# Streamed left operands of TensorE moved to multiples of 512 bytes: the pools of two projections of a decoder layer shifted and reordered

## The chip, the cores and the metric

The kernel runs on one core of a Trainium2 chip. The metric is the time of one execution in microseconds (us); three executions of the kernel before were timed, and their median stands for it.

## The reference

One decoder layer on 1024 tokens of width 1024, in float32, followed by a last RMSNorm:

```python
h = RMSNorm(x)
rnn_x, rnn_y, conv_B, conv_C, conv_x, gate_rnn, gate_conv = split(h @ w_in)   # 7 x 1024 columns
A = gelu(rnn_y) * RG_LRU(causal_conv4(rnn_x))     # two block-diagonal products in the gates
B = conv_B * causal_conv3(conv_C * conv_x)
x = x + (sigmoid(gate_rnn) * A + sigmoid(gate_conv) * B) @ w_out
x = x + (silu(n @ w_gate) * (n @ w_up)) @ w_down            # n = RMSNorm(x), hidden width 2816
x = x + sigmoid(RMSNorm(x) @ w_pg) * (p @ w_ple)
out = RMSNorm(x)
```

## The kernel before, in words

Every large product is done in float32 out of two halves: each operand is kept as a high and a low part (`split`, L83: ScalarE casts the high part, VectorE subtracts for the low one), and one product of tiles is three matmuls (`mm`, L108). Around this stands a scheme of seven block products instead of eight: the left matrix A and the right matrix B are cut into quarters, seven products of sums of quarters are made, and their results are added up in PSUM banks called X, Y and Z.

The stages follow one another: the transposed norm of x; the input projection, with the recurrence and the short convolution beside it; the output projection; gate and up; the down projection; the gate of the per-layer embedding and the last norm.

The input projection and gate/up are **streamed** (`stream`, L207). The weights are the left operand. They come in by DMA on SP's queue as quarters of 128x512 (`part`, pools `w1` and `w2`), are added up on VectorE (`source`, L232, with the tile `s1` of pool `ws`), cast by ScalarE (`high`, L248) and completed by VectorE (`low`, L253) into a tile `wop` of pool `wp` or, for the last two products of a later pair, of pool `wq`. The activations are the right operand: seven tiles of the pool `ops` made by `right_operands` (L173). They come from the norm of the second token half: `xt[4]` to `xt[7]` are scaled (L144), transposed on TensorE (L151, 32 transpositions), and VectorE and ScalarE read the transposed blocks (L190 and L192) into tiles `r` and `r_late`, out of which T1, T2, B22, T3 and -T4 are made (L86, L100). The two first products of the first four pairs need B11 and B21 alone, which are ready sooner; they run in front ("lead" products, 8 of 12 matmuls each). The first results are read out of PSUM into tiles of the pool `e0` (`z<-Z`, L514, in the input projection; `a<-Z`, L784, in gate/up); a bank comes free when that is done.

The output and down projections (`outer`, L336) have both operands in tiles of `ops`.

Where a tile lies in its partition follows from the pools: they are laid one behind the other in the order in which they are opened, behind what stays for the whole program. The pools of a stage (an `ExitStack`) take over the place of the pools of the stage before, and an instruction that writes a place waits for those that still use it. The stage before each stream has a `Frame` (L395) with pools `pq` (5 tiles of 8 KB), `pb` (4 of 4 KB: `xt[4]` to `xt[7]`), `pj`, `pa` (4 of 4 KB: `xt[0]` to `xt[3]`, then `r_late`) and `pr`, in that order. The table gives the places in bytes from the start of a partition.

| pool | before | rest to 512 | after | rest to 512 |
|---|---|---|---|---|
| Frame `pq` / `pb` / `pj` / `pa` | 132928 / 173888 / 190272 / 196416 | | the same | |
| `ops` (right operands everywhere; left ones in `outer`) | 17536 on | 128 | the same | 128 |
| `w1`, `w2`, `ws` | 132928 on | 320 | 133120 on | 0 |
| `wp`, 5 x 4096 | 153408 to 173888 | 320 | 153600 to 174080 | 0 |
| `wq`, 2 x 4096, gate/up | 190272 on | 320 | 174080 to 182272 | 0 |
| `wq`, input projection | 190400 on | 448 | 174080 to 182272 | 0 |
| `ev`, 4 x 2048 | 173888 on | 320 | 182272 on | 0 |
| `e0`, 4 tiles | 182080 on | 320 | 190464 on | 0 |

In the input projection the `e0` tiles are 2064 bytes, rounded to 2080; in gate/up 2048. The two block-diagonal products of the recurrence (`rg`) have their right operand `rg_w` in a tile of `wp` and their left one, `xo`, behind these pools; both go from rest 320 to 0 with the others.

The order in which a queue gets its instructions is the scheduler's: it simulates the program with the priorities of the code, so that another place, with other waits, can give another order.

Of the kernel before, what the change touches and what calls it, by code (L numbers as in the profile page):

```python
# [10 lines left out]
F32 = mybir.dt.float32  # L11
# [5 lines left out]
P = 128  # L17
T = 1024
D = 1024
H = 512  # L20
DFF = 2816
NF = DFF // P
EPS = 1e-6
LEAD = 4

# columns of the per-channel constants
C_W4, C_B4, C_BR, C_BI, C_LAM, C_W3, C_GM, C_GF, C_GP, NCST = 0, 32, 40, 48, 56, 64, 88, 96, 104, 112

# sections of the input projection
# [6 lines left out]
def kernel(ctx, tc, x, pT, w_in, w_gu, w_rg, w_out, w_down, w_pg, w_ple, cst, g_fin, out):  # L36
    """Float32 products run as float32r passes over exact 12-bit halves of the
    operands (lo*hi, hi*lo, hi*hi); the projections use Strassen's scheme in
    Winograd's form (seven block products in place of eight), whose running
    sums stay in PSUM:  # L40

        P1 = A11 B11    P2 = A12 B21    P3 = S4 B22    P4 = A22 (-T4)
        P5 = S1 T1      P6 = S2 T2      P7 = S3 T3
        S1 = A21 + A22  S2 = S1 - A11   S3 = A11 - A21   S4 = A12 - S2
        T1 = B12 - B11  T2 = B22 - T1   T3 = B22 - B12  -T4 = B21 - T2
        C11 = P1 + P2                   C12 = P1 + P6 + P5 + P3
        C22 = P1 + P6 + P7 + P5         C21 = P1 + P6 + P7 + P4

"""
# [33 lines left out]
    def split(hi, lo, src):  # L83
        """hi + lo == src, each with 12 significant bits."""
        nc.scalar.copy(hi, src)  # L85
        nc.vector.tensor_sub(lo, src, hi.bitcast(F32))  # L86

    def op_of(pieces, name):
        """A quarter of a matrix, given as pieces [P, k, H], as an operand."""
        t = ops.tile([P, 2, 4, H], F32R, tag="op", name=name)  # L90
        k = 0
        for q in pieces:
            n = q.shape[1]
            split(t[:, 0, k:k + n], t[:, 1, k:k + n], q)
            k += n
        return t
# [11 lines left out]
    def mm(ps, lhs, rhs, first, last, start):  # L108
        """ps (+)= lhs.T @ rhs; lhs and rhs give the two halves by index."""
        for n, (i, j) in enumerate(((1, 0), (0, 1), (0, 0))):  # L110
            nc.tensor.matmul(ps, lhs(i), rhs(j), start=start and first and n == 0,  # L111
                             stop=last and n == 2, skip_group_check=not start)

# [5 lines left out]
    root = [None]  # the last square root, behind which other tables may be loaded  # L119

    def rstd(ss, nb):
        """(sum of the parts / D + EPS) ** -0.5, with one Newton step behind the table."""
# [17 lines left out]
    def scale_rows(xt, y, spread):  # L140
        """xt[b] *= y[:, b]; spread: VectorE takes its share."""
        for b in range(4):
            if spread:
                nc.vector.tensor_scalar_mul(xt[b], xt[b], y[:, b:b + 1])  # L144
            else:
                nc.scalar.activation(xt[b], xt[b], AF.Copy, scale=y[:, b:b + 1])
# [7 lines left out]
    def norm_half(xt, ss, gc, piece, spread):  # L154
        """xt: four [P, D] tiles (overwritten), ss: their sums of squares. Returns the two quarters
        of (norm(x) * g).T for the first and second half of D, in pieces [P, 2, H]. spread: VectorE
        takes its share."""
# [15 lines left out]
    def right_operands(r11, r21, xt, ss, gc, piece, held=0):  # L173
        """The seven right operands in the order of use: B11, B21, T1, T2, B22, T3, -T4, from the
        quarters of the first token half and the blocks of the second (as for norm_half). The sums
        overwrite the quarters. held: so many banks of PSUM are taken for the products that follow
        before the transpositions take theirs."""
# [5 lines left out]
        second = []  # L183
# [20 lines left out]
    def stream_pools(st):  # L204
        return {n: pool(st, n, bufs) for n, bufs in (("w1", 4), ("w2", 4), ("ws", 2), ("wp", 5), ("ev", 4), ("e0", LEAD), ("wq", 2))}

    def stream(pools, srcs, hops, banks, take, pump=lambda: None, ahead=2, early=0):  # L207
        """srcs: raw rows of each pair of channel blocks. take(n)(blk, half, psum, sb): takes
        psum + sb, block blk of pair n on token half half. pump(): called behind each product."""
        n_pairs = len(srcs)  # L210
        # Two pairs run interleaved, so that a sum in PSUM is read three products before it goes
        # on; the first pairs run the products of the first token half in front.
# [11 lines left out]
        def part(q, i, j):  # L224
            """Quarter A(i, j) of pair q."""
            if (q, i, j) not in parts:
                t = pools["w%d" % i].tile([P, 4, P], F32, tag="w", name="part")
                dma[0] = nc.sync.dma_start(out=t, in_=srcs[q][i - 1][:, 4 * (j - 1):4 * j])
                parts[q, i, j] = t
            return parts[q, i, j]  # L230

        def source(q, i):  # L232
            """What becomes the left operand of product i of pair q; the sums overwrite the quarters."""
# [25 lines left out]
        def advance(n):  # L259
            """What is due before product n: the steps of an operand lie one product apart, the  # L260
            last ahead of its use by a few."""
# [48 lines left out]
    def deferred(work=()):  # L310
        """later(n, fn): fn runs n products from now (at once for 0). work: generators, of which
        the first goes a step with each product."""
# [23 lines left out]
    def outer(a, b, s1, nk, acc, after=lambda i: None, mid=lambda: None):  # L336
        """a, b: the four quarters of the operands as dicts of pieces (the sums overwrite them).
        after(i): called behind the results of product i."""
        def prep(i):
# [4 lines left out]
            if i == 5:  # L344
                each(add, s1, a[1, 0], a[1, 1])
                each(sub, b[0, 0], b[0, 1], b[0, 0])                       # T1
                return op_of(s1, "s1"), op_of(b[0, 0], "t1")
            if i == 6:
                each(sub, a[1, 0], a[0, 0], a[1, 0])                       # S3
                each(sub, a[0, 0], s1, a[0, 0])                            # S2  # L350
                each(sub, b[0, 0], b[1, 1], b[0, 0])                       # T2
                return op_of(a[0, 0], "s2"), op_of(b[0, 0], "t2")
            if i == 3:
                each(sub, a[0, 1], a[0, 1], a[0, 0])                       # S4
                return op_of(a[0, 1], "s4"), op_of(b[1, 1], "b22")
            if i == 7:
                each(sub, b[0, 1], b[1, 1], b[0, 1])                       # T3
                return op_of(a[1, 0], "s3"), op_of(b[0, 1], "t3")
            each(sub, b[1, 0], b[1, 0], b[0, 0])                           # -T4
# [28 lines left out]
    def load(pieces, src, r0, c0, eng=nc.sync):  # L388
        """src[r0:, c0:c0 + H] into pieces [P, k, H]."""
# [5 lines left out]
    class Frame:  # L395
        """Memory of the phases around a norm: tiles of x, quarters of its transposition, and
        quarters of the operands."""
# [32 lines left out]
    def residual(xt, ss, fr, last, store):  # L430
        """acc and after of outer: x += product; on the last round sums of squares, and the
        finished halves go out."""
# [20 lines left out]
    # ================= p @ w_ple; norm of x =================  # L453
    with ExitStack() as st:
# [5 lines left out]
        # pieces [P, 2, H] of [P, 2, 1024] by column halves  # L460
# [34 lines left out]
    # ================= input projection, recurrence, short conv =================  # L495
    with ExitStack() as st:
# [19 lines left out]
        def halo(sec, h, blk, width):  # L516
            """The columns before each half: zeros, then the end of the first half."""
# [7 lines left out]
        def recurrence(h):  # L525
            """In steps, one per product of the projection: what a step reads has been issued
            by the steps before it."""
            prev = [None, None]
            for half in range(2):
# [71 lines left out]
                for blk in range(2):  # L601
                    # 1 - a^2 = (1 + a^2) * tanh(-log a)
# [17 lines left out]
        def softplus():  # L620
            # 8 * softplus(-lambda) = 8 * (max(-lambda, 0) + log1p(exp(-|lambda|)))
# [9 lines left out]
            # log1p(e) = 2 atanh(s), s = e / (2 + e) <= 1/3  # L631
# [23 lines left out]
        def gate_v(h, blk, half):  # L655
            """conv * conv_b * sigmoid(gate), as the factors arrive."""
# [8 lines left out]
        def taker(h, sec):  # L665
# [22 lines left out]
            def use(t, *key):  # L688
# [12 lines left out]
                elif sec == GR:  # L701
                    hs = need(("h", *key))
                    # the next half still starts from the last column of this one
# [27 lines left out]
    # ================= output projection, residual, norm =================  # L731
# [36 lines left out]
    # ================= SwiGLU: gate and up =================  # L768
    with ExitStack() as st:
# [6 lines left out]
        def swiglu(f):  # L776
            def take(blk, half, psum, sb):
                # blk 0: gate, blk 1: up
# [21 lines left out]
    # ================= SwiGLU: down, residual, norm, ple gate, final norm =================  # L800
    with ExitStack() as st:
# [43 lines left out]
        def op_in_x(pieces, name):  # L845
            """An operand in the place of four tiles of x."""
# [13 lines left out]
        def gate(b, dh, left, cuts=1, last=False):  # L860
            """Token block b, half dh of the columns, in as many pieces as cuts."""
# [56 lines left out]
def _columns(a):  # L918
    """Per-channel rows [..., 1024] as columns [128, rows * 8]: channel = block * 128 + partition."""
# [4 lines left out]
def _pair_rows(w):  # L924
    """[1024, pairs, 2, 128] as [pairs, 2, 128 rows of a block, 8 blocks, 128 columns]."""
# [4 lines left out]
def _arrays(x, p, g_mix, w_in, conv4_w, conv4_b, w_rg_r, b_rg_r, w_rg_i, b_rg_i, lru_lambda, conv3_w, w_out,  # L930
# [4 lines left out]
    rg = np.stack([n(w_rg_r)[0], n(w_rg_i)[0]])  # [gate, head, i, j]  # L935
# [33 lines left out]
```

## Time and profile before

| | us |
|---|---|
| median of the three runs | 1463.45 |
| lowest, highest | 1461.16, 1463.68 |
| span of the profiled execution (first to last instruction) | 1458.2 |
| TensorE busy in it | 1437.6 |
| VectorE busy | 1077.8 |
| ScalarE busy | 781.7 |

The profile gives no time of the profiled execution other than its span. Its mean granted TensorE clock is 0.997. Times in the rows below are us from the start of that span. PE is TensorE's matmul, PEld its weight load, which overlaps the matmul before it; DVE is VectorE, ACT ScalarE. "idle before <-" names what an engine waited for. The end of a matmul is modelled, so the distance between two starts is the safer measure: from the first start of one row to the first start of the next, divided by the matmuls of the row.

### The profile page before, as it was taken

Reading aid. Unit: us, or ns where it says so; the run is one execution under the profiler, and the core shown is the slowest. Engines: PE = TensorE matmul, PEld = TensorE weight load, DVE = VectorE, ACT = ScalarE, POOL = GpSimd, SP = SyncE. Lnnn points to the kernel's source line nnn. Section 1 sums busy time; section 2 is a strip of 40 time slices with the busy share of each in tenths; the row PEclk is TensorE's granted clock in tenths of the full one; section 3 lists DMA queues with packets and bytes.
Section 4 is the critical chain, followed back from the end, with each engine's and each line's share of the span. In section 5 each row is a group of like instructions: output and inputs, shape, how many; then the busy total and the mean of one; then the engine's idle time right before and its main releaser. Section 6 shows DMA issues by size and latency. Waiting matters only on the chain.

```text
span 1458.2 us, 17521 instructions
## 1 busy us (share of the span) xinstructions
PE 1437.6 (99%) x6348; PEld 1176.0 (81%) x6348; DVE 1077.8 (74%) x1617; ACT 781.7 (54%) x1214; POOL 10.6 (1%) x20
## 2 busy tenths in 40 slices
PE   8999999999999999999999999999999999999997
PEld 6787888888888888878888888888888888888886
DVE  6989757965697669689796555555554899995854
ACT  7757746754775467545773333333333343346764
POOL 0000000000000000000000000000000000000000
PEclk9999999999999999999999999999999999999999
DMA  8321221122112211381522222222223761524431
GB/s 317 111 87 51 75 77 52 52 79 74 53 55 75 77 51 59 111 286 53 172 81 101 87 82 85 87 88 83 76 80 106 255 231 37 195 87 141 148 145 58
DMA packets 76742, 153.77 MB, mean 105 GB/s; under 512 B 7920, under 2 KB 7920, under 8 KB 76656
## 3 DMA queue, kind: packets, MB, share of 16 engines
q1 hardware_dynamic: 74768, 145.84, 29.9%
q0 software_dynamic: 1888, 6.82, 1.4%
q8 instruction: 50, 0.82, 0.2%
q14 instruction: 36, 0.29, 0.1%
HBM read 120.12 MB, written 32.51 MB: 105 GB/s over the span
## 4 chain that ended last, share of the span: by engine, by line
PE 90%; DVE 3%; DMA 3%; ACT 2%; issue 1%; SPq 0%; DVEq 0%; ACTq 0%
PE X L111 46%; PE Y L111 23%; PE Z L111 11%; PE pg L874 6%; PE rg L111 3%; PE tp L151 1%; DMA pe_d<-peo 1%; DMA xt<-x_d 1%; DMA xt<-in_x 0%; ACT b L85 0%; DVE a11b L100 0%; DMA act_d<-a 0%; DMA a<-m_d 0%; DMA m_d<-v 0%; DVE v L722 0%
## 5 line engine op out<-in xcount | busy, mean ns | idle before, releaser
L111 PE MATMUL X<-t,wop 128*128 128x512 f32 x1800 | 431.3, 393 | 0.0
L111 PEld LDWEIGHTS X<-t,wop 128*128 128x128 f32 x1800 | 338.2, 188 | 76.6 <-DVE wop L254 0.3
L250 ACT CAST wop<-part 128x512 fp32r<-128x512 f32 x300 | 183.7, 621 | 213.8 <-PE X L111 67.4
L254 DVE TENSOR_TENSOR wop<-part,wop 128x512 fp32r<-128x512 f32 x300 | 204.8, 689 | 89.0 <-ACT wop L250 87.8
L111 PE MATMUL Z<-b,wop 128*128 128x512 f32 x600 | 146.7, 393 | 0.4 <-ACT r_late L192 0.4
L111 PE MATMUL X<-b,wop 128*128 128x512 f32 x600 | 147.0, 393 | 0.0
L111 PE MATMUL Y<-b,wop 128*128 128x512 f32 x600 | 146.4, 393 | 0.0
L111 PE MATMUL Y<-t,wop 128*128 128x512 f32 x600 | 146.2, 393 | 0.0
L111 PEld LDWEIGHTS Z<-b,wop 128*128 128x128 f32 x600 | 112.5, 188 | 26.8 <-ACT r_late L192 0.9
L111 PEld LDWEIGHTS Y<-b,wop 128*128 128x128 f32 x600 | 112.8, 188 | 25.5
L111 PEld LDWEIGHTS Y<-t,wop 128*128 128x128 f32 x600 | 112.8, 188 | 25.2
L111 PEld LDWEIGHTS X<-b,wop 128*128 128x128 f32 x600 | 112.6, 188 | 24.6
L874 PE MATMUL pg<-b,a 128*128 128x512 f32 (+1 forms) x408 | 88.4, 378 | 0.0
L111 PE MATMUL X<-t,s 128*128 128x512 f32 x360 | 85.8, 392 | 0.0
L874 PEld LDWEIGHTS pg<-b,a 128*128 128x128 f32 x408 | 73.4, 188 | 14.6
L254 DVE TENSOR_TENSOR wop<-s,wop 128x512 fp32r<-128x512 f32 x50 | 34.5, 689 | 59.5 <-ACT wop L250 59.5
L111 PEld LDWEIGHTS X<-t,s 128*128 128x128 f32 x360 | 66.8, 188 | 13.9 <-DVE t L86 0.5
L271 ACT COPY p<-Y 128x512 f32<-128x512 f32 x50 | 29.2, 583 | 72.6 <-PE Y L111 72.6
L271 ACT COPY s<-X 128x512 f32<-128x512 f32 x50 | 29.2, 588 | 59.2 <-PE X L111 58.9
L271 ACT COPY u<-X 128x512 f32<-128x512 f32 x50 | 29.2, 584 | 49.6 <-PE X L111 49.1
L435 DVE TENSOR_TENSOR xt<-X,xt 128x512 f32<-128x512 f32 x64 | 43.8, 686 | 14.5 <-PE X L111 13.6
L111 PE MATMUL rg<-xo,rg_w 128*128 128x512 f32 x192 | 47.1, 393 | 0.1
(172 smaller groups left out, 1939.7 us busy)
## 6 DMA issues: line engine op xcount, KB each, us to landing
part<-in_w_in SPq DMA_DIRECT2D x120, 256.0 KB, 2.6
part<-in_w_gu SPq DMA_DIRECT2D x96, 256.0 KB, 2.7
act_d<-a SPq DMA_DIRECT2D x44, 256.0 KB, 2.4
x_d<-xt SPq DMA_DIRECT2D x32, 256.0 KB, 2.0
bc<-in_w_down SPq DMA_DIRECT2D x10, 512.0 KB, 5.8
a<-act_d SPq DMA_DIRECT2D x10, 512.0 KB, 5.9
xt<-in_x SPq DMA_DIRECT2D x8, 512.0 KB, 8.0
pe_d<-peo SPq DMA_DIRECT2D x16, 256.0 KB, 2.9
```

The lines of the kernel that those rows point to most:

```text
L111: nc.tensor.matmul(ps, lhs(i), rhs(j), start=start and first and n == 0, stop=last and n == 2, skip_group_check=not start)
L151: nc.tensor.transpose(ps[:, b * P:(b + 1) * P], xt[b][:, kk * P:(kk + 1) * P], ident)
L250: nc.scalar.copy(t[:, 0], s)
L254: sub(t[:, 1], s, t[:, 0].bitcast(F32))
L271: nc.scalar.copy(t, ps)
L435: add(piece, ps, piece)
L874: nc.tensor.matmul(ps, left[k // 4](i, k % 4)[:, c:c + P], right[k // 4, dh][:, j, k % 4, r], start=n + k == 0, stop=n == 2 and k == 7)
```

## The change

One pool of 192 bytes that nothing uses is opened ahead of the others, and `wq` is opened behind `wp` instead of last. (All comments were dropped too, so that lines behind L203 are two higher in the new file.)

```diff
     def stream_pools(st):
-        return {n: pool(st, n, bufs) for n, bufs in (("w1", 4), ("w2", 4), ("ws", 2), ("wp", 5), ("ev", 4), ("e0", LEAD), ("wq", 2))}
+        pool(st, "rest", 1).tile([P, 48], F32, name="rest")
+        return {n: pool(st, n, bufs) for n, bufs in (("w1", 4), ("w2", 4), ("ws", 2), ("wp", 5), ("wq", 2), ("ev", 4), ("e0", LEAD))}
```

No engine has an instruction more or fewer. Their order differs at the starts of the two streams. TensorE at the start of gate/up, before (`tp` is a bank with transposed blocks, `b_5936` is B11, `b_5941` B21, `t_5998` T1):

```order
L111 MATMUL X<-t_5659,a_5654 128x512 x43
L111 MATMUL X<-b_5936,wop 128x512 x22
L151 MATMUL tp<-ident,xt 128x128 x5
L111 MATMUL X<-b_5936,wop 128x512
L151 MATMUL tp<-ident,xt 128x128 x15
L111 MATMUL X<-b_5936,wop 128x512 x7
L151 MATMUL tp<-ident,xt 128x128 x4
```

and after the change (B11 is `b_5941` now, B21 `b_5946`, T2 `t_6038`, T1 `t_6003`):

```order
L111 MATMUL X<-t_5664,a_5659 128x512 x45
L151 MATMUL tp<-ident,xt 128x128 x32
L111 MATMUL X<-b_5941,wop 128x512 x12
L111 MATMUL Z<-b_5946,wop 128x512 x12
...
L111 MATMUL X<-t_6038,wop 128x512 x12
L111 MATMUL Y<-t_6003,wop 128x512 x12
```

The transpositions, which stood among the first products, stand ahead of them. VectorE at the same place, before:

```order
L137 SCALAR_TENSOR_TENSOR rz<-rt,ry 128x4
L254 TENSOR_TENSOR wop<-part,wop 128x512
L144 TENSOR_SCALAR xt<-xt,rz 128x1024 x4
L245 TENSOR_TENSOR part<-part 128x512
L190 SCALAR_TENSOR_TENSOR r<-tp,cs,r 128x512 x2
...
L254 TENSOR_TENSOR wop<-part,wop 128x512
L784 TENSOR_TENSOR a<-Z,s_6119 128x512
L190 SCALAR_TENSOR_TENSOR r<-tp,cs,r 128x512 x3
```

and after the change, with the first lo-halves of `wop` (L256 now) and, further down, the first sums out of PSUM (L786 now):

```order
L144 TENSOR_SCALAR xt<-xt,rz 128x1024 x4
L190 SCALAR_TENSOR_TENSOR r<-tp,cs,r 128x512 x4
L86 TENSOR_TENSOR t_6003<-r,t_6003 128x1024
L190 SCALAR_TENSOR_TENSOR r<-tp,cs,r 128x512 x2
L256 TENSOR_TENSOR wop<-part,wop 128x512 x4
...
L86 TENSOR_TENSOR b_6050<-r_late,b_6050 128x1024
L100 TENSOR_TENSOR r<-r 128x1024
L786 TENSOR_TENSOR a<-Z,s_6128 128x512
```

The first lo-half moved from ahead of the scaling of `xt` to behind six steps of L190, and the first `a<-Z` from among them to behind both halves of B22. At the start of the input projection VectorE makes the four `z` sums, which stood apart among the steps for T2, T3 and B22, in one row behind them:

```order
L86 TENSOR_TENSOR b_492<-r_late,b_492 128x1024 x2
L100 TENSOR_TENSOR r<-r 128x1024
L516 TENSOR_TENSOR z<-Z,s_574 128x512
L516 TENSOR_TENSOR z<-Z,s_614 128x512
L516 TENSOR_TENSOR z<-Z,s_665 128x512
L516 TENSOR_TENSOR z<-Z,s_702 128x512
```

There `b_492` is B22, and the order of TensorE's first products stays as it was.

## Rows read from the trace of the kernel before

**Rows 1.** The page, part 1: busy us, share of the span, instructions.
```profile
PE 1437.6 (99%) x6348; PEld 1176.0 (81%) x6348; DVE 1077.8 (74%) x1617; ACT 781.7 (54%) x1214; POOL 10.6 (1%) x20
```

**Rows 2.** The page, part 4: the chain that ended last, by engine.
```profile
PE 90%; DVE 3%; DMA 3%; ACT 2%; issue 1%; SPq 0%; DVEq 0%; ACTq 0%
```

**Rows 3.** Stretches in three stages: length, PE, PEld, DVE, ACT, POOL, clock, DMA, GB/s.
```profile
1180.00:1330.00 150.00, 150.00 (x663) 124.23 (x662) 143.97 (x156) 60.90 (x71) 5.76 (x8) 1.00 0.41 136
760.00:1150.00 390.00, 390.00 (x1706) 320.05 (x1705) 229.36 (x333) 144.60 (x244) 2.54 (x4) 1.00 0.30 98
150.00:620.00 470.00, 470.00 (x2032) 381.65 (x2031) 350.94 (x557) 283.90 (x441) 0.00 (x0) 1.00 0.21 69
```

**Rows 4.** Timeline of TensorE in the input projection: start, length, operation.
```profile
339.30 2.96 PE L111 MATMUL Y<-b,wop 128*128 128x512 f32 x12
342.10 5.76 PE L111 MATMUL X<-t,wop 128*128 128x512 f32 x24
347.70 2.96 PE L111 MATMUL Y<-t,wop 128*128 128x512 f32 x12
...
361.65 5.66 PE L111 MATMUL X<-t,wop 128*128 128x512 f32 x24
367.14 2.91 PE L111 MATMUL Y<-t,wop 128*128 128x512 f32 x12
```

**Rows 5.** The two streams in their steady parts, columns as in rows 3.
```profile
77.43:633.79 556.36, 556.21 (x2401) 451.05 (x2400) 421.75 (x684) 343.52 (x531) 1.56 (x2) 1.00 0.23 73
748.29:1143.81 395.52, 395.52 (x1729) 324.52 (x1728) 234.64 (x339) 148.20 (x249) 2.54 (x4) 1.00 0.29 94
```

**Rows 6.** Groups of weight loads: busy us, mean ns, idle before.
```profile
L111 PEld LDWEIGHTS Y<-t,wop 128*128 128x128 f32 x600 | 112.8, 188 | 25.2
L111 PEld LDWEIGHTS X<-t,s 128*128 128x128 f32 x360 | 66.8, 188 | 13.9 <-DVE t L86 0.5
```

**Rows 7.** Timeline of TensorE at the start of gate/up.
```profile
716.08 5.20 PE L111 MATMUL X<-b,wop 128*128 128x512 f32 x22
721.32 0.74 PE L151 MATMUL tp<-ident,xt 128*128 128x128 f32 x5
...
745.54 2.91 PE L111 MATMUL Y<-t,wop 128*128 128x512 f32 x12
```

**Rows 8.** Timeline of VectorE there.
```profile
716.28 0.69 DVE L435 TENSOR_TENSOR xt<-X,xt 128x512 f32<-128x512 f32 x1
...
719.82 0.69 DVE L254 TENSOR_TENSOR wop<-part,wop 128x512 fp32r<-128x512 f32 x1
720.43 2.73 DVE L144 TENSOR_SCALAR xt<-xt,rz 128x1024 f32<-128x1024 f32 x4
```

**Rows 9.** Timeline of ScalarE there.
```profile
728.01 1.06 ACT L85 CAST t<-r 128x1024 fp32r<-128x1024 f32 x1
```

**Rows 10.** Timeline of VectorE near 58 us, steps back to back.
```profile
58.00 0.69 DVE L243 TENSOR_TENSOR part<-part 128x512 f32<-128x512 f32 x1
58.60 1.22 DVE L100 TENSOR_TENSOR r_late<-r_late 128x1024 f32<-128x1024 f32 x1
59.73 0.69 DVE L254 TENSOR_TENSOR wop<-s,wop 128x512 fp32r<-128x512 f32 x1
```

**Rows 11.** Stretches before the first stream, columns as in rows 3.
```profile
38.00:41.00 3.00, 1.38 (x10) 1.07 (x11) 3.00 (x5) 1.64 (x4) 0.00 (x0) 0.99 0.93 326
41.00:44.30 3.30, 3.15 (x16) 2.67 (x15) 3.30 (x7) 2.56 (x6) 0.00 (x0) 0.50 0.26 99
```

**Rows 12.** Waits of TensorE: us in total, times, longest.
```profile
PE Z L111 <- DVE a L86: 2.1, 1, 2.1
```

**Rows 13.** Timeline of TensorE at the first `rg` product.
```profile
97.03 2.93 PE L111 MATMUL rg<-xo,rg_w 128*128 128x512 f32 x12
99.79 2.97 PE L111 MATMUL X<-t,wop 128*128 128x512 f32 x12
```

## The prediction, written before the result was known

> **What bounds the kernel now.** I read the page's busy times first, then the chain that ended last, then the stretches of TensorE one by one. TensorE is busy 99% of the span [rows 1] and holds 90% of the chain [rows 2]. So only two things can move the time: the distance from one matmul to the next, and places where TensorE has no product to start.
>
> The distance is not the same everywhere, and that is what the change is about. In the output and down projections (outer products, left operands in the `ops` pool) 662 weight loads stand in 150 us: 226.6 ns each. In gate/up 1705 stand in 390 us: 228.7 ns. In the input projection 2031 stand in 470 us: 231.4 ns [rows 3]. The clock is 1.00 in all three and the work is the same 128x512 matmul. What differs is where the left operand begins in its partition. By the sizes of the pools, an `ops` tile begins 128 bytes past a multiple of 512, a `wp` tile 320 bytes past one, a `wq` tile 320 past in gate/up but 448 past in the input projection, since there the four `z` tiles ahead of it are 2,064 bytes, rounded to 2,080. The right operands are the same `ops` tiles in all three. Row by row in the input projection, two products side by side run at 2.80 us per twelve matmuls (339.30 to 342.10, and 342.10 to 347.70 for 24): 233.3 ns; later ones at 5.49 us for 24 (361.65 to 367.14): 228.8 ns [rows 4]. By the operands that stand there, the slow period begins with products from `wq` and lasts over products from `wp` behind them until the next pair from `wq`. So the trace orders three places: 128 gives 226.6, 320 gives 228.8, 448 gives 233.3 and slows its neighbours. It shows no stream of 128x512 products at 0.
>
> **The change, part by part.** It adds and removes no instruction on any engine. It does two things.
>
> *The places.* All left operands of the two streams go to 0. The stretch from the first steady product of the input projection to the first outer product has 2400 weight loads in 556.36 us, 231.8 ns each; the one of gate/up has 1728 in 395.52 us, 228.9 ns each [rows 5]. Nothing in the trace prices place 0. The bounds: from above the 233.3 ns of the worst place (a loss of 2400 x 1.5 + 1728 x 4.4 = 11.2 us); from below a pace under all that the trace shows. The nearest row to that is the weight load's own duration, 188 ns [rows 6]; nothing comes near it, and a third of the way from 226.6 towards it (214) is as far as I would go, a gain of 4128 x 16.6 = 68 us. I take the value of place 128, 226.6 ns: the pace falls steadily from 448 over 320 to 128, place 0 is next to 128, and 226.6 is flat in its stretch, matmul after matmul, as if the place no longer mattered there. Gain: 2400 x 5.2 = 12.5 us, less 0.6 us of short stalls in that stretch which stay, so 11.9; and 1728 x 2.3 = 4.0 us. Together **-15.9 us**.
>
> *The order of the starts.* The pools also come to lie over other tiles of the stage before. Before, `wp` (20 KB) lay wholly over `pq`, whose tiles are done early. Now its fifth buffer reaches 192 bytes into `xt[4]`, and `wq` lies over `xt[4]` and `xt[5]`: weights for the first products wait until the second token half has been transposed. `e0` now lies over `pj` and the first `r_late` tile, so that the first sums out of PSUM wait until T3 and B22 have been made.
>
> At the start of gate/up, products on B11 began at 716.08, with the 32 transpositions let in between them, and the first Y followed at 745.54 [rows 7]. Now all 32 transpositions stand ahead of the first product. Chain: the last `xt` sum ends at 716.97; the scaling of `xt` starts at 720.43 behind a lo-half [rows 8], so at 719.8 without it, and takes 2.7; four steps of L190 take 2.6 more, to 725.2; then ScalarE's casts of t1 (1.06 us, [rows 9]), its `r_late` steps and the first `wop` cast, to 728.5, and the lo-half on VectorE, to about 729.4. TensorE meanwhile has only the transpositions, 13.3 us in place of products that took the same time before. Eight lead products at 2.72 us bring it to 751.2, the one on T2 to 753.9. Y needs a bank of PSUM, which comes free with the first `a<-Z` sum on VectorE. That one now stands behind ten 128x1024 steps, two of L190 and sixteen 128x512 ones counted from 731.0. Back to back the long and the short ones take 1.13 and 0.60 us [rows 10]: 11.3 + 1.3 + 9.6 = 22.2, to 753.2, and with 1.7 us, an estimate, for casts that ScalarE brings late, 754.9. Against 745.54 that is 9.4 us; I take **+10 us**, because the clock may be at half while TensorE only transposes: before the first stream, behind 3 us in which TensorE was busy for 1.38, it was 0.50 over 3.3 us of transpositions [rows 11], and such a stretch is 1.65 us of work lost. Bounds: 8.4 (TensorE's own chain, VectorE in time) less whatever slack I misjudged, say 5; and 13.3 + 1.7 = 15, nothing made good.
>
> At the start of the input projection the transpositions already stood ahead of the products, which start about where they did. There only the `z` sums move: all four now stand behind the lo-halves of T3 and B22 and the sums for T4. The first Y waits for them until about 72.2, with TensorE ready at 70.7. I take **+1.4 us**, between 0 and 3.
>
> At both ends of the streams, the loads of the next stage stand where they stood on SP's queue, or ahead of the last stores; TensorE's one wait there, 2.1 us for `a` [rows 12], hangs on the last `m_d` store and stays. Cost nothing; if that cover fails it is one load, under 3 us.
>
> **Sum:** -15.9 + 10 + 1.4 = -4.5 us. The profiled execution's span is 1458.2 us; the median of the runs is 1463.45, so some 5 us lie outside the span, and I take them as unchanged. 1463.45 - 4.5 gives **1459.0**.
>
> The Trainium skill bears on the first term. The page "TensorE: Matmul & The Clock Gate" (Part 2, step 1, LDWEIGHTS) says that the load of the left operand has a read port of its own and that its time depends on the number of columns alone. By that rule the start address changes nothing and the sum would be +11.4. The trace agrees for the load's own time, 188 ns in every group [rows 6], but the pace differs at the same columns and clock [rows 3], and there the measurement decides.
>
> **The rivals.**
>
> *The pace does not follow the place that way (slower).* Then only the starts are left: 1463.45 + 11.4 = 1474.9. For it: the correlation rests on three places, each in its own stage, and `rg`, whose two operands both begin at 320, takes 2.76 us per twelve (97.03 to 99.79), 230 ns [rows 13], about what `wp` has. What may count is the distance between left and right operand: 0 gives 226.6, 192 gives 228.8, 320 gives 233.3, and the change makes it 384, worse than all. `rg` at distance 0 but not at 226.6 speaks against that. At 233.3 everywhere: 11.2 more, 1486. The rival decides from the point where the pace gains no more than the starts lose: 11.4 us over 4128 matmuls, 2.8 ns, that is a mean of 227.8 against 230.6 before. Chance 0.22.
>
> *Place 0 is better than 128.* The 512 bytes of a weight load that begins on a multiple of 512 lie in one piece of that size; from place 128, as from 320 and 448, they lie in two. If the pace went to 220, another 4128 x 6.6 = 27 us: 1432. Against it: 226.6 is flat, and a price on the second piece would show at 128, 320 and 448 alike. Chance 0.16. The same page of the Trainium skill gives a gap of 512 / 2.4 + 2.5 = 216 ns between such matmuls (Part 2, "Back-to-back issue gap"); by it the time would be near 1415, and no row here shows that pace.
>
> *The starts cost nothing.* If VectorE catches up and TensorE's first products only move, -15.9 stands alone: 1447.6. Against it: 13.3 us of products have to come from somewhere, and TensorE has no idle time behind in which to make them good. Chance 0.08, within the forecast's 0.62 of a pace near 226.6.
>
> **How the numbers follow.** Forecast (pace 226 to 227, gate/up start 5 to 15): 0.62, 1454 to 1464. Pace rival above 0.22, pace rival below 0.16. The range runs from 1445 (the forecast with free starts and a little more pace) to 1475 (no gain in pace at all). It leaves out a pace well under 225 and one worse than now, together about 0.2. A measurement of this kernel tells about 0.2% from no change, 2.9 us. Faster by more: 0.16 and six tenths of the forecast's case, 0.53. Slower by more: nearly all of 0.22 and a little of the forecast, 0.24. The same: 0.23.
>
> **What would show it.** Right: in the profile of the changed kernel the stretches of both streams have one even distance near 226.6 ns, the input projection takes 12 us less than 556.36 and gate/up 4 less; TensorE shows 32 transpositions in a row near 722 to 729, the first product near 729 and Y near 755. Wrong: a distance of 228.8 or more with the operands at 0, which is the first rival; or products among the transpositions, which would make the starts cheaper than I say.

## The result and the profile after

The changed kernel takes 1485.08 us (median of four runs) where the kernel before took 1462.43 in the same comparison: a ratio of 1.0163, 95% interval 1.0148 to 1.0179. It is slower by 22.7 us; the forecast was 1459.0, that is 4.5 us faster.

The page of the changed kernel, span, parts 1 and 4, to set beside [rows 1, 2]:

```profile
span 1482.2 us, 17509 instructions
...
PE 1452.0 (98%) x6348; PEld 1179.5 (80%) x6348; DVE 1079.5 (73%) x1617; ACT 782.5 (53%) x1214; POOL 10.6 (1%) x20
...
PE 91%; DVE 4%; DMA 2%; ACT 1%; issue 1%; POOL 0%; SPq 0%; DVEq 0%; ACTq 0%
```

TensorE is the bound as before, and has become slower itself: 14.4 us more of busy time for the same 6348 matmuls. (The page of before counts 17521 instructions; each engine's own count is the same, the difference lies in instructions on semaphores.) The steady parts of the two streams (columns as in rows 3), to set beside [rows 5]:

```profile
78.08:637.36 559.28, 559.23 (x2402) 450.38 (x2400) 420.87 (x673) 342.50 (x529) 1.56 (x2) 1.00 0.23 72
765.70:1167.26 401.56, 401.56 (x1730) 325.55 (x1728) 230.51 (x335) 147.53 (x250) 2.55 (x4) 1.00 0.28 92
```

That is 233.0 ns a matmul in the input projection (231.8 before) and 232.4 in gate/up (228.9 before), at a clock of 1.00. The pace is not 226.6. Row by row in the input projection the fast stretches of [rows 4] are gone; product after product takes 2.80 us for twelve matmuls, 233.3 ns each:

```profile
343.95 5.76 PE L111 MATMUL X<-t,wop 128*128 128x512 f32 x24
349.55 2.96 PE L111 MATMUL Y<-t,wop 128*128 128x512 f32 x12
```

The start of gate/up on TensorE, to set beside [rows 7]:

```profile
712.84 10.49 PE L111 MATMUL X<-t,a 128*128 128x512 f32 x45
727.25 6.77 PE L151 MATMUL tp<-ident,xt 128*128 128x128 f32 x32 [3.92 <-DVE xt L144]
736.15 4.62 PE L111 MATMUL X<-b,wop 128*128 128x512 f32 x12 [2.12 <-DVE wop L256]
...
762.91 2.95 PE L111 MATMUL Y<-t,wop 128*128 128x512 f32 x12
```

The last product of the output projection ends at about 712.84 + 45 x 0.2267 = 723.04 (716.08 before, where the first `wop` product followed at once). All 32 transpositions stand alone, with idle time on both sides, and the granted clock falls with it: its mean is 0.57 over the transpositions and 0.62 over the first product behind them, so that most of both stretches was at the lower of its two levels, 0.50 (1.2 GHz):

```profile
722.00:727.25 5.25, 1.33 (x7) 0.79 (x5) 3.11 (x10) 1.13 (x5) 0.00 (x0) 0.91 0.26 100
727.25:734.10 6.85, 6.77 (x32) 5.82 (x32) 5.80 (x9) 3.66 (x6) 0.00 (x0) 0.57 0.00 0
...
736.15:740.60 4.45, 4.45 (x12) 3.50 (x13) 4.45 (x6) 3.37 (x6) 0.00 (x0) 0.62 0.71 214
```

Cut at the same places of the program, the 24.0 us between the two spans lie as follows:

| piece | before, us | after, us | difference |
|---|---|---|---|
| to the first steady product of stream 1 | 77.43 | 78.08 | +0.65 |
| stream 1, 2400 matmuls | 556.36 | 559.28 | +2.92 |
| output projection | 82.29 | 85.68 | +3.39 |
| start of gate/up | 32.21 | 42.66 | +10.45 |
| gate/up, 1728 matmuls | 395.52 | 401.56 | +6.04 |
| the rest | 314.35 | 314.95 | +0.60 |

The 3.39 us at the output projection were not expected. There GpSimd, ScalarE, VectorE, SP's queue and TensorE wait for one another in turn. It begins with the load of B21 of `w_out` (`b<-in_w_out`), which GpSimd issues. Before and after the change (the long wait is only that GpSimd has nothing else to do):

```profile
625.92 1.56 POOL L392 DMA_DIRECT2D b<-in_w_out  x2 [624.61 <-DMA bc<-in_w_out]
```

```profile
632.23 1.56 POOL L394 DMA_DIRECT2D b<-in_w_out  x2 [630.92 <-DVE b L86]
```

ScalarE of the changed kernel waits for that load to land:

```profile
634.31 1.03 ACT L85 CAST a<-a 128x1024 fp32r<-128x1024 f32 x1
639.65 1.05 ACT L85 CAST b<-b 128x1024 fp32r<-128x1024 f32 x1 [4.30 <-DMA b<-in_w_out]
641.71 1.05 ACT L85 CAST b<-b 128x1024 fp32r<-128x1024 f32 x1 [1.00 <-DMA b<-in_w_out]
642.66 0.62 ACT L687 ACTIVATE z<-z 128x512 f32<-128x512 f32 x1
```

And TensorE waits further down, in the kernel before and in the changed one:

```profile
652.45 5.73 PE L111 MATMUL Z<-b,a 128*128 128x512 f32 x24 [2.15 <-DVE a L86]
```

```profile
648.28 5.60 PE L111 MATMUL Z<-b,a 128*128 128x512 f32 x24
657.73 7.36 PE L111 MATMUL Z<-b,a 128*128 128x512 f32 x24 [3.85 <-DVE a L86]
```

By the sizes of the pools the load goes into the last tile of `pq`, at 165696. Before, that place was two `wop` buffers exactly; shifted by 192 bytes, the end of a third one lies in it too. The load was issued at 625.92 before, 7.87 us ahead of the stage's first product (633.79), and now 5.13 us ahead of it (632.23 against 637.36): 2.74 us later, about one product of 2.80. In both kernels the issue stands 0.47 us behind the start of a product of the stream, the third from the end before (625.45) and the second from the end now (631.76). That it waits for the product in front of that one is inferred from this; the profile names other steps as what ended the wait. ScalarE waits for it with the sigmoid of the last `z` (642.66) queued behind; so the last store to `m_d` and the load of `a` come late, and TensorE waits 3.85 us for it instead of the 2.1 of [rows 12]. Behind the gap 24 matmuls take 7.20 us (657.73 to 664.93, clock 0.76) instead of 5.57 (652.45 to 658.02, clock 1.00):

```profile
657.70:664.93 7.23, 7.20 (x24) 5.76 (x25) 5.54 (x8) 1.47 (x5) 0.00 (x0) 0.76 0.55 206
```

One correction to the part on the kernel: in the `rg` products `rg_w` is the left operand and `xo` the right one, and both lie in tiles of `wp`. So their distance is 0 in every kernel here.

### The profile page after: what moved, and what is told of

It reads as the page before. It is cut to its first block, busy times and chain, and to the rows that moved or that the text cites. A ratio compares the mean times of both kernels' runs of the same rounds, so it can differ in the third digit from the quotient of the medians.

```text
span 1482.2 us, 17509 instructions
## 1 busy us (share of the span) xinstructions
PE 1452.0 (98%) x6348; PEld 1179.5 (80%) x6348; DVE 1079.5 (73%) x1617; ACT 782.5 (53%) x1214; POOL 10.6 (1%) x20
## 4 chain that ended last, share of the span: by engine, by line
PE 91%; DVE 4%; DMA 2%; ACT 1%; issue 1%; POOL 0%; SPq 0%; DVEq 0%; ACTq 0%
PE X L111 47%; PE Y L111 23%; PE Z L111 11%; PE pg L876 6%; PE rg L111 3%; PE tp L151 1%; DMA pe_d<-peo 1%; DMA b<-in_w_out 1%; PE ple L111 1%; DMA prow<-in_pT 0%; DVE t L86 0%; DMA a<-m_d 0%; DVE xt L437 0%; DVE wop L256 0%; DVE v L724 0%
## 5 line engine op out<-in xcount | busy, mean ns | idle before, releaser
L256 DVE TENSOR_TENSOR wop<-part,wop 128x512 fp32r<-128x512 f32 x300 | 204.2, 689 | 94.3 <-ACT wop L252 92.8
L256 DVE TENSOR_TENSOR wop<-s,wop 128x512 fp32r<-128x512 f32 x50 | 34.5, 689 | 60.6 <-ACT wop L252 60.5
L111 PE MATMUL Z<-b,a 128*128 128x512 f32 x180 | 43.4, 400 | 3.9 <-DVE a L86 3.9
```

Of the source, the lines that this page charges most:

```text
L256: sub(t[:, 1], s, t[:, 0].bitcast(F32))
```

## The experiments

Below, the place of an operand is where it begins, in bytes past a multiple of 512. Theory A: the pace follows the distance from the right operand's place to the left one's. Theory B, the prediction's: it follows the left operand's own place. The streams and the outer products of before and after have four places of the left operand and only one of the right (128), so they can't tell. The right operands (and both operands of the outer products) can be moved without moving anything else: some or all of the 704 bytes of small tiles (pool `sm`) go ahead of `ops` instead of behind it, so that all behind them stays where it was. "z tiles of 2176" means that the early `z` tiles are padded, so that `wq` has the same place as `wp` in both streams.

**E1, all at 320.**

```diff
-    ops = ctx.enter_context(tc.tile_pool(name="ops", bufs=7))
     sm = ctx.enter_context(tc.tile_pool(name="sm", bufs=2))
+    ops = ctx.enter_context(tc.tile_pool(name="ops", bufs=7))
...
-            return (sp["e0"] if early else zp).tile([P, H + 4], F32, tag="z", name=name)
+            return (sp["e0"] if early else zp).tile([P, H + (32 if early else 4)], F32, tag="z", name=name)[:, :H + 4]
```

> The kernel before with the small pool opened ahead of the pool of the right operands, and early z tiles of 2176 bytes: all left and right operands of 128x512 products begin 320 past a multiple of 512, order of every engine as before. Theory A (the pace follows the distance from the right operand's place to the left one's, modulo 512; distance 0 is fast): 226.6 ns in both streams, about 1446.5 us. Theory B (the pace follows the left operand's own place): 228.8 ns in both streams and 228.8 instead of 226.7 in the outer products, about 1458.6 us.

Measured: 1445.85 us against 1460.17, ratio 0.9894 (0.9877 to 0.9911). The two streams:

```profile
75.28:620.50 545.22, 544.75 (x2401) 450.36 (x2400) 421.22 (x685) 342.20 (x531) 1.56 (x2) 1.00 0.23 74
735.25:1126.93 391.68, 391.68 (x1730) 324.43 (x1728) 234.88 (x339) 148.28 (x249) 2.55 (x4) 1.00 0.29 95
```

227.2 and 226.7 ns, in gate/up with the left operands exactly where they were. B falls. And the first `rg` product, whose operands have not moved at all against each other:

```profile
94.32 2.88 PE L111 MATMUL rg<-xo,rg_w 128*128 128x512 f32 x12
97.04 2.88 PE L111 MATMUL X<-t,wop 128*128 128x512 f32 x12
```

2.72 us for twelve, 226.7 ns, where [rows 13] show 2.76: there its neighbours were slow, here they are fast. Start by start, the trace of before shows the slow neighbour wear off within that product: the first distance is 240 ns, and from the eighth start to the twelfth (98.650 to 99.557) they stand 226.7 ns apart.

**E2, right operands at 448.** As E1, but only `rv`, `rs`, `ry`, `rt`, `rz` go ahead of `ops`:

```diff
-    ops = ctx.enter_context(tc.tile_pool(name="ops", bufs=7))
-    sm = ctx.enter_context(tc.tile_pool(name="sm", bufs=2))
+    sa, ops, sb = (ctx.enter_context(tc.tile_pool(name=n, bufs=b)) for n, b in (("sa", 2), ("ops", 7), ("sb", 2)))
+    sm = type("Small", (), {"tile": lambda *a, name, **k: (sa if name in ('rv', 'rs', 'ry', 'rt', 'rz') else sb).tile(*a, name=name, **k)})
```

> The kernel before with the right operands moved from 128 to 448 by putting some of the small tiles ahead of them, left operands of the streams all at 320, order of every engine as before. Distance 384, as after the change, but no tile lies over another one than before. Theory A: 232.4 to 233.3 ns in both streams, as after the change; 226.7 in the outer products, where both operands move together; about 1472 us. Theory B: 228.8 ns in the streams, 233 in the outer products, whose left operands are at 448; about 1466 us.

Measured: 1472.24 us, ratio 1.0077 (1.0058 to 1.0095).

```profile
78.23:637.44 559.21, 559.14 (x2401) 450.40 (x2400) 421.60 (x684) 344.34 (x531) 1.56 (x2) 1.00 0.22 73
752.08:1155.28 403.20, 403.20 (x1729) 324.38 (x1728) 235.31 (x339) 148.32 (x249) 2.54 (x4) 1.00 0.28 92
...
1200.00:1320.00 120.00, 120.00 (x532) 99.34 (x531) 117.47 (x126) 46.94 (x53) 4.33 (x6) 1.00 0.35 120
```

In the outer products (last row), whose two operands are at 448 here, 531 loads stand in 120 us, 226.0 ns, where theory B expected 233. The streams take 233.0 and 233.3 ns: the slow pace without any change to left operands, pools of the streams or order. This is the pace part of the loss by itself.

**E3, the order of the pools alone.**

```diff
-        pool(st, "rest", 1).tile([P, 48], F32, name="rest")
```

(taken out of the changed kernel).

> The changed kernel without the 192 bytes: wq ahead of ev and e0, left operands at 320 in both streams, right ones at 128 (distance 192). Both theories: 228.8 ns in both streams, 7 us less than before. If the new order of the pools alone makes the starts late (wq over xt[4] and xt[5], e0 over pj and the first r_late): first product of gate/up near 736 us, and about 14 us lost, 1469 us. If it is the 192 bytes by which wp reaches into xt[4]: products among the transpositions as before, about 1456 us.

Measured: 1456.55 us against 1460.17, ratio 0.9973 (0.9960 to 0.9987). TensorE at the start of gate/up:

```profile
708.20 5.20 PE L111 MATMUL X<-b,wop 128*128 128x512 f32 x22
713.44 0.73 PE L151 MATMUL tp<-ident,xt 128*128 128x128 f32 x5
...
741.15 3.03 PE L111 MATMUL Y<-t,wop 128*128 128x512 f32 x12 [0.57 <-DVE a L785]
```

Products stand among the transpositions as in [rows 7], the first 82.1 us behind the first outer product. The 0.57 us that Y waits for a sum of `a` is what the new place of `e0`, over `pj` and `r_late`, seems to cost. Stream 1 takes 550.70 us, 229.5 ns, now that `wq` is no longer at 448.

**E4, all at 0.** The changed kernel, split as in E2 with `ss` ahead of `ops` as well:

```diff
+    sm = type("Small", (), {"tile": lambda *a, name, **k: (sa if name in ('rv', 'rs', 'ry', 'rt', 'rz', 'ss') else sb).tile(*a, name=name, **k)})
```

> The changed kernel with the right operands moved from 128 to 0 as well: left and right operands of the streams and of the outer products all begin on multiples of 512; order of every engine as in the changed kernel. Theory A: 226.6 ns in both streams, 25 us less than the changed kernel, about 1460 us. Theory B: streams as in the changed kernel (232.4 to 233.3 ns), outer products slower too, about 1495 us.

Measured: 1461.6 us, ratio to before 1.0007 (0.9995 to 1.0019).

```profile
76.67:621.91 545.24, 544.75 (x2401) 450.22 (x2400) 420.27 (x673) 340.33 (x529) 1.56 (x2) 1.00 0.23 74
749.74:1141.50 391.76, 391.76 (x1730) 324.38 (x1729) 230.55 (x335) 147.89 (x250) 2.55 (x4) 1.00 0.29 94
```

Same left operands as in the changed kernel, same order on every engine, and a span that is 24.6 us shorter (1457.6). What is left is the late starts, paid for by the better pace.

**E5, the shift alone.** The old order of the pools, `z` tiles of 2176, and

```diff
     def stream_pools(st):
+        pool(st, "rest", 1).tile([P, 48], F32, name="rest")
```

> The kernel before with only the 192 bytes ahead of the streams' pools (and early z tiles of 2176 bytes, so that wq is at 0 too); the pools stay in their old order, so ev and e0 lie over xt and wq over pj and pa, as before. Left operands at 0, right ones at 128 (distance 384). Pace 232.4 to 233.3 ns in both streams. Theory S (the 192 bytes by which wp now reaches into xt[4], and the parts into the next tile, make the starts late): first product of gate/up behind all 32 transpositions, about 98 us behind the first outer product as in the changed kernel, about 1485 us. Rival (wq over xt and e0 over pj and r_late are needed for that as well): first product about 82 us behind it, as before, about 1471 us.

Measured: 1484.99 us, ratio 1.0171 (1.0149 to 1.0194), as slow as the changed kernel. TensorE:

```profile
728.87 6.77 PE L151 MATMUL tp<-ident,xt 128*128 128x128 f32 x32 [3.92 <-DVE xt L144]
737.77 4.61 PE L111 MATMUL X<-b,wop 128*128 128x512 f32 x12 [2.13 <-DVE wop L255]
```

The first product stands 98.7 us behind the first outer product (639.10). So the 192 bytes make this start late, and the new order of the pools is not needed for it.

**E6, E7, E8: how the distance counts.** As E2, left operands at 320, with other names in the list, so that the right ones are at 64, 256 and 384:

```diff
-    ... name in ('rv', 'rs', 'ry', 'rt', 'rz') ...
+    ... name in ('rv', 'rs', 'ry', 'rt', 'rz', 'fss') ...
+    ... name in ('rv', 'rs') ...
+    ... name in ('rv', 'rs', 'ry', 'rt') ...
```

> The kernel before with all left operands of the streams at 320 and the right ones at 64 (distance 256), order of every engine as before. If the distance counts modulo 256: 226.7 ns as at distance 0, about 1446 us. If it counts modulo 512: something else, between the 228.9 of distance 192 and the 233.3 of distance 320, about 231 ns, 1463 us.

```profile
737.35:1129.03 391.68, 391.68 (x1729) 324.32 (x1728) 234.62 (x339) 148.31 (x249) 2.55 (x4) 1.00 0.29 95
```

> The kernel before with all left operands of the streams at 320 and the right ones at 256 (distance 64), order of every engine as before. Modulo 256: 233.3 ns as at distance 320, about 1472 us. Modulo 512: next to distance 0, 226.7 to 228.9 ns, 1446 to 1455 us.

```profile
751.21:1154.41 403.20, 403.20 (x1730) 325.25 (x1728) 235.04 (x339) 148.40 (x249) 2.54 (x4) 1.00 0.29 92
```

> The kernel before with all left operands of the streams at 320 and the right ones at 384 (distance 448, or 64 the other way), order of every engine as before. Modulo 256: 228.9 ns as at distance 192, about 1455 us. Modulo 512: between the 233 of distance 384 and the 226.7 of distance 0, about 230 ns, 1460 us. If only the size of the gap counted and not its side, the same as at distance 64.

```profile
744.63:1140.14 395.51, 395.51 (x1729) 324.52 (x1728) 234.82 (x340) 148.34 (x249) 2.54 (x4) 1.00 0.29 93
```

Gate/up at 226.7, 233.3 and 228.9 ns, one run each of 1445.03, 1471.0 and 1456.06 us: all three as expected if the distance counts modulo 256.

**E10, E11: between the places.** Distances 32 and 224:

```diff
+    ... name in ('rv', 'rs', 'warm') ...
+    ... name in ('rv', 'rs', 'ry', 'rt', 'rz', 'fss', 'warm') ...
```

> The kernel before with all left operands of the streams at 320 and the right ones at 288 (distance 32), order of every engine as before. If the pace changes in steps of 64 bytes or more: 226.7 ns, 1445 us. If it changes smoothly: about 230 ns, between the 226.7 of distance 0 and the 233.3 of distance 64, 1459 us. If the best place is beside 0: below 226.7 ns.

```profile
753.60:1156.80 403.20, 403.20 (x1730) 324.65 (x1728) 235.20 (x339) 148.36 (x250) 2.55 (x4) 1.00 0.28 92
...
1200.00:1330.00 130.00, 130.00 (x576) 107.66 (x575) 127.06 (x136) 53.96 (x61) 4.34 (x6) 1.00 0.35 119
```

> The kernel before with all left operands of the streams at 320 and the right ones at 96 (distance 224), order of every engine as before. Steps of 64 bytes: 228.9 ns as at distance 192, 1456 us. Smooth: about 227.8 ns, 1451 us. If the best place is beside 0: below 226.7 ns.

```profile
754.72:1157.91 403.19, 403.19 (x1730) 323.84 (x1728) 234.94 (x339) 148.25 (x250) 2.54 (x4) 1.00 0.28 92
```

Both 233.3 ns (1473.47 and 1474.53 us, one run each), and none of my three expectations. The fast place is distance 0 itself; 32 bytes to either side of it the pace is the slow one. In the same kernel E10 the outer products, whose operands move together, keep 575 loads in 130 us, 226.1 ns (last row).

**E12, `wp` first.** E5 with

```diff
-        ... (("w1", 4), ("w2", 4), ("ws", 2), ("wp", 5), ("ev", 4), ("e0", LEAD), ("wq", 2))}
+        ... (("wp", 5), ("w1", 4), ("w2", 4), ("ws", 2), ("ev", 4), ("e0", LEAD), ("wq", 2))}
```

> The kernel with only the 192 bytes ahead of the streams' pools, old order of the pools but with wp opened first, ahead of w1, w2 and ws: all left operands at 0 and right ones at 128 as in the changed kernel (distance 384), but now it is the second tile of ws that reaches 192 bytes into xt[4], and no tile wop does. Pace 232.4 to 233.3 ns in both streams. If the reach of wp into xt[4] is what made the start of gate/up late: first product among the transpositions, 10 us of the start come back, about 1474 us, of which 3 may come back too if the late load at the start of the output projection also goes. If any shift by 192 bytes makes the start late: 1485 us.

Measured: 1471.5 us against 1461.74, ratio 1.0075 (1.0058 to 1.0093).

```profile
716.81 5.28 PE L111 MATMUL X<-b,wop 128*128 128x512 f32 x22
721.95 1.34 PE L151 MATMUL tp<-ident,xt 128*128 128x128 f32 x10
```

Gate/up there, and the load of B21:

```profile
752.18:1153.74 401.56, 401.56 (x1729) 326.13 (x1728) 236.18 (x341) 149.71 (x252) 2.54 (x4) 1.00 0.28 94
```

```profile
616.99 1.56 POOL L393 DMA_DIRECT2D b<-in_w_out  x2 [615.69 <-DMA a11b<-in_w_out]
```

Left operands at 0, the same shift, the slow pace (gate/up 401.56 us again), and products among the transpositions: the shift as such does not make the start late. What E5 has and E12 has not is the reach of `wp` into `xt[4]`. (`w1`, `w2` and `ws` lie elsewhere too; that one of them matters was not tested by itself.) The load of B21 is issued early too, 17.75 us ahead of the first outer product (634.74), and TensorE's wait for `a` is 1.9 us. From the first outer product to the steady part of gate/up it is 117.4 us (634.74 to 752.18), where E5 has 128.2 (639.10 to 767.32) and the kernel before 114.5 (633.79 to 748.29): 10.8 of 13.7 us come back. Of the 2.9 us that stay, 1.4 is a longer wait for `r_late` (1.8 us, 0.4 before), and about 1.6 the clock behind it: 36 matmuls take 10.01 us (731.02 to 741.03, clock 0.83) where the twelve behind them take 2.79.

**E9, a version better than both.** The changed kernel without the 192 bytes and with `sm` opened ahead of `ops`: no padding, all operands at 320.

```diff
-    ops = ctx.enter_context(tc.tile_pool(name="ops", bufs=7))
     sm = ctx.enter_context(tc.tile_pool(name="sm", bufs=2))
+    ops = ctx.enter_context(tc.tile_pool(name="ops", bufs=7))
...
-        pool(st, "rest", 1).tile([P, 48], F32, name="rest")
```

> Candidate for the best version: the new order of the pools without the 192 bytes, and the small pool ahead of the pool of the right operands, so that all 128x512 operands begin at 320 (distance 0) and no part, wop or xt reaches into a neighbour's tile; no padding of the z tiles is needed. 226.7 ns in both streams, first product of gate/up among the transpositions; 1445 us, like the version that keeps the old order. If the order of the pools costs something by itself, 1 to 2 us more than that.

Measured: 1445.45 us against 1460.85, ratio 0.9889 (0.9872 to 0.9905).

```profile
739.61:1131.42 391.81, 391.81 (x1728) 324.54 (x1729) 233.08 (x339) 150.23 (x253) 2.56 (x4) 1.00 0.29 95
```

It can't be told from E1. Both beat the kernel before by 14 to 15 us and the changed one by some 39.

Gate/up over all runs, 1728 matmuls (E3's stretch is 741.15 to 1136.79):

| right, left place | distance mod 256 | us | ns |
|---|---|---|---|
| 320, 320 (E1, E9); 0, 0 (E4); 64, 320 (E6) | 0 | 391.68, 391.81; 391.76; 391.68 | 226.7 |
| 288, 320 (E10) | 32 | 403.20 | 233.3 |
| 256, 320 (E7) | 64 | 403.20 | 233.3 |
| 128, 0 (after, E5, E12) | 128 | 401.56 | 232.4 |
| 448, 320 (E2) | 128 | 403.20 | 233.3 |
| 128, 320 (before, E3); 384, 320 (E8) | 192 | 395.52, 395.64; 395.51 | 228.9 to 229.0 |
| 96, 320 (E11) | 224 | 403.19 | 233.3 |

The distance is not all that counts. In the input projection of before the products from `wp` all have distance 192, and yet those behind one pair from `wq` (distance 64 modulo 256) take 2.80 us per twelve and those behind the next pair 2.75 [rows 4]. And at places 128 and 0 the changed kernel takes 233.3 ns through most of its input projection but 232.4 in gate/up. So at distances other than 0 something else has a part, and what ran just before is the nearest candidate; this was not followed. At distance 0 every stream here ran at 226.7 ns, and 227.2 with the short stalls of the input projection.

## Why the prediction was wrong, step by step

**What bounds the kernel: right.** TensorE's pace and the places without a product were all that moved.

**The places: wrong, and this decided it.** The step was "the pace falls steadily from 448 over 320 to 128, place 0 is next to 128", with 226.6 ns for place 0. -15.9 us were forecast and 2.92 + 6.04 = +9.0 measured. In the trace of before every stream has its right operands at 128, so that the place of the left operand and its distance from the right one were the same variable; I chose one and priced it as a trend through three points. At place 0 the streams ran at 233.0 and 232.4 ns, and E1, E2 and E4 show that the pace follows the distance between the two operands. The first rival named that and its time, 1486, and got 0.22. I set it aside because `rg`, at distance 0, ran at 230 ns. Those were twelve matmuls between slow neighbours; the last ones among them already ran at 226.7, and in E1 all do. The rival was right in kind and wrong in one point: 384 was not "worse than all", it equals 128 modulo 256. That its 1486 lies so near the measured 1485.08 is in part luck: the pace cost 9.0 us and not the rival's 11.2, and what stands outside the streams' steady parts cost 15.1 and not 11.4.

**The start of gate/up: right in size, with another last step.** +10 forecast, +10.45 measured. Taken 6.96 us back for what was late already (723.04 - 716.08), the first product starts at 729.2 (729.4 forecast) and Y at 755.95 (754.9). But Y waited for TensorE's own chain and not, as forecast, for VectorE's sum `a<-Z`: the first of the four sums is done near 762.4, and Y follows its X at 762.91 without a wait. TensorE's own chain was 8.4 in the forecast; the clock added 1.66 and the slower pace of nine products 0.6. VectorE's rows:

```profile
726.35 2.74 DVE L144 TENSOR_SCALAR xt<-xt,rz 128x1024 f32<-128x1024 f32 x4
...
735.41 2.49 DVE L256 TENSOR_TENSOR wop<-part,wop 128x512 fp32r<-128x512 f32 x4
...
761.75 2.48 DVE L786 TENSOR_TENSOR a<-Z,s 128x512 f32<-128x512 f32 x4
```

The half clock came, too, and cost its time in the first product, which takes 4.45 us (736.15 to 740.60) instead of 2.79; the transpositions themselves were done before the first `wop`. The reason was too wide: of the three overlays I named, E5 and E12 together put it on `wp` over `xt[4]`, and E3 that `wq` over `xt` and `e0` over `r_late` cost 0.6 us at most.

**The start of the input projection: too dear.** +1.4 forecast, +0.65 measured, and 0.50 of that is the slower pace of the lead products (33.56 us against 33.06 from the first to the steady one). The first Y did not wait: it followed its X at 71.35. My sum of VectorE's steps was too long there: the four `z` sums start at 70.00.

**The ends of the streams: wrong.** "Cost nothing" was forecast, with "one load, under 3 us" if the cover fails. It failed: 3.39 us, of which 1.75 are the longer wait and 1.6 the clock behind it. I had compared the order on SP's queue, which had not changed, and not what each load waits for; the one that came late is issued by GpSimd. E12, where `wp` lies elsewhere, has the load early and a wait of 1.9 us again.

**The base: a misreading without effect.** I put 5 us between the time and the span. In the runs of the changed kernel and of the experiments they are 1.8 us apart (1483.98 and 1482.2 in the profiled one); the rest of the 5 was the difference between executions. It cancels in the forecast.

**The rule weighed.** The Trainium skill, page "TensorE: Matmul & The Clock Gate" (Part 2, step 1), says that loading the next left operand takes no read bandwidth from the running matmul. The load's own time agrees: 188 ns in gate/up of E1 and of E2 (324.43 and 324.38 us for 1728). The pace is not the same, as it would be by that rule: 226.7 and 233.3 ns in the same two, where only the right operands have moved. There the measurement decides; it does not show whether the load is what costs the time. The 216 ns that the prediction takes from the Trainium skill are, in the section that it names, the gap of an isolated matmul; no stretch here comes near it, the fastest take 226.0 (outer products of E2) and 226.7 (gate/up of E1).

## What to carry to other kernels

A place that is good for one operand alone may not exist: move both operands of the matmul and look at their distance, here modulo 256 bytes, before aligning anything. Of the six distances tried here, from 0 to 224, only 0 gave 226.7 ns. A trend over stages in which one other thing stays fixed is not a price; a run that moves only the other thing (here 704 bytes of small tiles) costs little and tells them apart. When a pool moves by any number of bytes, list which tiles of the next and the last stage it now touches: 192 bytes cost nearly 14 us at two starts here (10.45 and 3.39).

## What was not expected of the hardware

The fast place is narrow: distances of 32 and 224 bytes give the full 233.3 ns, 192 gives 228.9, 0 gives 226.7. In gate/up distance 128 gives 232.4 at places 128 and 0 but 233.3 at 448 and 320; since the input projection of the changed kernel has 233.3 at 128 and 0 too, that need not be the absolute place. Why the distance counts was not shown: no run here separates the load of the next left operand from the reading of the right one. The mean granted clock was 0.76 behind a wait of 3.85 us and 0.57 while TensorE only transposed, and each time a part of the next products ran at the lower level: 1.6 us lost in each case.
